# A two-layer decoder step on one core: each weight quarter's products in two passes, high part first

## The chip, the cores and the metric

The kernel runs on one core of a Trainium2 chip. The metric is the device time of the whole launch in microseconds (us), a median of several runs. Engines are named as in the profile: PE is TensorE, PEld its weight load, DVE is VectorE, ACT is ScalarE, POOL is GpSimd, SP is SyncE, which issues most of the transfers.

## What is computed

Two layers of a hybrid decoder trunk for 256 prompt tokens and 8 single decode tokens, 264 token columns in all. Cut to what matters here, a layer is

```
h = rms_norm(x) * norm_w
z = h @ w_in                      # (264, 2048) @ (2048, 7296)
A = rwkv_time_mix(z[:, :3200])    # 12 heads, a recurrent matrix state, a triangular solve per chunk
B = dilated_attention(z[:, 3200:6272])
C = pooling(z[:, 6272:])
x = x + concat(A, B, C) @ w_out   # (264, 2048) @ (2048, 2048)
```

All inputs and outputs are float32.

## The kernel before, in words

**The two large products.** Activations lie with channels on the partitions and the 264 tokens along the free dimension. `stream` (line 301) multiplies them by a group of output tiles of 128 columns, mostly two at a time (`nt` = 2), one PSUM accumulator `acc` for each. The 2048 input channels are taken in four quarters of 512 (loop over `q`), and each quarter in four pieces of 128 (loop over `k4`). To keep float32 accuracy with the faster matmul type, every operand is split into a high part, which is the operand rounded to that type, and a low part, the difference. For a quarter, one transfer brings the weights into `raw` (three buffers, line 294), ACT makes `hi` from it (line 137 is the helper), DVE makes `lo` = `raw` - `hi` (helper, line 140). `hi` and `lo` have two buffers each. For each tile and each piece PE then does three products into the same accumulator: `hi` with the high activations `xh`, `hi` with the low ones `xl`, `lo` with `xh` (line 320). In the output projection the activations are named `mh`, `mb`, `mc` for the high parts and `ml` and others for the low ones. A quarter of a two-tile group is thus 24 matmuls, 12 for each tile, and a layer has 28 such groups and one of a single tile in the input projection (57 tiles) and 8 groups in the output projection: 7008 matmuls in the two layers.

The accumulators come from a PSUM pool `acc` of three banks (line 184, `setup`). A group takes two. When a group ends, DVE reads both (`scaled`, line 326, writes `z`; the output projection's loop in `late` writes `xs`), and the next group's second tile needs the bank that this group's first tile leaves.

**The side work.** Everything else (time mixing, attention, pooling, norms) is small matmuls in the PSUM pool `a` and element work on DVE, ACT and POOL, which is to run beside the streams.

**The order.** The program order written by `Trunk` is not what the engines run. `Plan` (line 1321) reads all instructions, their dependences and the buffers of each pool, gives each a cost, and lists them anew for every engine (`run`, line 1503). An instruction's priority is the length of the longest path behind it (`tails`, line 1478), in which the matmuls of the streams form one chain in program order. An engine takes the ready instruction of highest priority. Side matmuls go ahead of stream matmuls. A matmul whose buffer is not free is set aside and the next ready one is taken (`take`, line 1564). The order found is fixed: each engine then works through its list and waits at semaphores.

The very first group (`begin`) makes its activations quarter by quarter on the way (`first_x`, line 274, four `xh` on ACT and four `xl` on DVE for each quarter).

Of the kernel before, what the change touches and what calls it, by code (L numbers as in the profile page):

```python
# [19 lines left out]
P = 128  # L20
# [3 lines left out]
T = NP + NB  # L24
# [79 lines left out]
class Trunk:  # L104
# [196 lines left out]
    def stream(self, w, c0, nt, xh, xl, order=(0, 1, 2, 3), begin=False):  # L301
        n = nt * P
        accs = [self.ps("acc") for _ in range(nt)]
        for q in order:
            if begin:
                self.first_x(q)
                xh, xl = self.xh, self.xl
            raw = self.early.pop(0) if self.early else self.load(w, c0, n, q)
            hi = self.wpool.tile([P, 4, 256], F32R, tag="hi", name=self.nm("hi"), bufs=2)
            lo = self.wpool.tile([P, 4, 256], F32R, tag="lo", name=self.nm("lo"), bufs=2)  # L310
            self.act(hi[:, :, :n], raw[:, :, :n])
            self.tt(lo[:, :, :n], raw[:, :, :n], hi[:, :, :n].bitcast(F32), ALU.subtract)
            for t in range(nt):
                cs = slice(t * P, (t + 1) * P)
                for k4 in range(4):
                    k = 4 * q + k4
                    o = accs[t][:, :T]
                    first, last = q == order[0] and k4 == 0, q == order[3] and k4 == 3
                    for i, (a, b) in enumerate(((hi[:, k4, cs], xh[k]), (hi[:, k4, cs], xl[k]), (lo[:, k4, cs], xh[k]))):
                        self.nc.tensor.matmul(o, a, b, start=first and i == 0, stop=last and i == 2)  # L320
        return accs

    def project(self, tiles):
# [1439 lines left out]
```

## Time and profile before

| what | value |
|---|---|
| median of 3 runs | 1121.82 us (1119.73 to 1126.0) |
| the profiled execution's own time | 1125.52 us |
| span of that execution | 1123.7 us |
| mean granted TensorE clock, as a share of full speed | 0.977 |
| busy share of the span | PE 94%, PEld 90%, DVE 79%, ACT 49%, POOL 23% |
| stream matmuls (line 320) | 7008 of PE's 9802 |

The span runs from the first to the last instruction. The time of a launch has 1.8 us around it in this execution. PE's matmuls overlap each other, so its busy time counts pipelined work; idle time before an instruction is what its engine waited.

### The profile page before, as it was taken

Reading aid. Unit: us, or ns where it says so; the run is one execution under the profiler, and the core shown is the slowest. Engines: PE = TensorE matmul, PEld = TensorE weight load, DVE = VectorE, ACT = ScalarE, POOL = GpSimd, SP = SyncE. Lnnn points to the kernel's source line nnn. Section 1 sums busy time; section 2 is a strip of 40 time slices with the busy share of each in tenths; the row PEclk is TensorE's granted clock in tenths of the full one; section 3 lists DMA queues with packets and bytes.
Section 4 is the critical chain, followed back from the end, with each engine's and each line's share of the span. In section 5 each row is a group of like instructions: output and inputs, shape, how many; then the busy total and the mean of one; then the engine's idle time right before and its main releaser. Section 6 shows DMA issues by size and latency. Waiting matters only on the chain. (4 is left out here: it accounts for less than half of the span.)

```text
span 1123.7 us, 24664 instructions
## 1 busy us (share of the span) xinstructions
PE 1060.4 (94%) x9802; PEld 1009.0 (90%) x9802; DVE 889.4 (79%) x1665; ACT 545.4 (49%) x928; POOL 258.8 (23%) x391
## 2 busy tenths in 40 slices
PE   8999999889899999999999999988898999989998
PEld 7899999788898897999999999978788999879998
DVE  7668977799997897765675799679899989886444
ACT  6546533345446563444555564334473555634332
POOL 3202310465524111000120132005564321000000
PEclk9999999899999999999999999999898999999999
DMA  7554479866377875576765545897653679456764
GB/s 255 176 166 149 151 251 235 225 151 183 99 214 188 294 231 185 157 232 214 231 214 183 172 132 188 229 251 176 159 172 125 220 242 307 155 167 197 240 219 150
DMA packets 146651, 221.48 MB, mean 197 GB/s; under 512 B 67440, under 2 KB 100608, under 8 KB 146520
## 3 DMA queue, kind: packets, MB, share of 16 engines
q1 hardware_dynamic: 137272, 193.78, 56.9%
q0 software_dynamic: 9264, 26.13, 7.5%
q8 instruction: 77, 1.26, 0.5%
q14 instruction: 38, 0.31, 0.1%
HBM read 197.47 MB, written 22.95 MB: 196 GB/s over the span
## 5 line engine op out<-in xcount | busy, mean ns | idle before, releaser
L320 PE MATMUL acc<-xh,lo 128*128 128x264 f32 x1824 | 534.0, 294 | 27.3 <-DVE lo L140 26.7
L320 PE MATMUL acc<-xh,hi 128*128 128x264 f32 x1824 | 533.0, 293 | 8.2 <-ACT hi L137 7.8
L320 PE MATMUL acc<-xl,hi 128*128 128x264 f32 x1824 | 530.7, 291 | 3.6 <-DVE xl L149 3.6
L137 ACT ACTIVATE hi<-raw 128x1024 fp32r<-128x1024 f32 (+1 forms) x296 | 310.0, 1047 | 408.7 <-PE acc L320 308.0
L140 DVE TENSOR_TENSOR lo<-raw,hi 128x1024 fp32r<-128x1024 f32 (+1 forms) x296 | 361.3, 1221 | 162.1 <-ACT hi L137 159.9
L320 PEld LDWEIGHTS acc<-xh,lo 128*128 128x128 f32 x1824 | 349.8, 192 | 38.8 <-DVE lo L140 33.8
L320 PEld LDWEIGHTS acc<-xh,hi 128*128 128x128 f32 x1824 | 351.4, 193 | 14.4 <-ACT hi L137 8.9
L320 PEld LDWEIGHTS acc<-xl,hi 128*128 128x128 f32 x1824 | 351.3, 193 | 9.7 <-DVE xl L149 4.1
L320 PE MATMUL acc<-mb,hi 128*128 128x264 f32 x384 | 71.8, 283 | 0.0
L140 DVE TENSOR_TENSOR z<-acc,rstd 128x264 f32<-128x264 f32 (+1 forms) x112 | 52.1, 466 | 12.9 <-PE acc L320 12.2
L320 PEld LDWEIGHTS acc<-mb,hi 128*128 128x128 f32 x384 | 59.4, 188 | 0.0
L320 PE MATMUL acc<-mb,lo 128*128 128x264 f32 x192 | 54.6, 284 | 0.0
L320 PE MATMUL acc<-ml,hi 128*128 128x264 f32 x192 | 54.6, 284 | 0.0
L320 PE MATMUL acc<-mh,lo 128*128 128x264 f32 x192 | 54.5, 284 | 0.0
L320 PE MATMUL acc<-mh,hi 128*128 128x264 f32 x192 | 54.4, 283 | 0.0
L350 POOL COPY zcol<-z 128x9 f32<-128x9 f32 x50 | 21.1, 423 | 135.2 <-DVE z L140 132.4
L320 PE MATMUL acc<-mc,hi 128*128 128x264 f32 x256 | 47.6, 284 | 0.0
L320 PEld LDWEIGHTS acc<-mc,hi 128*128 128x128 f32 x256 | 39.7, 188 | 0.0
L320 PE MATMUL acc<-mc,lo 128*128 128x264 f32 x128 | 36.6, 286 | 0.0
L320 PEld LDWEIGHTS acc<-mh,hi 128*128 128x128 f32 x192 | 36.1, 188 | 0.0
L320 PEld LDWEIGHTS acc<-mh,lo 128*128 128x128 f32 x192 | 36.1, 188 | 0.0
L320 PEld LDWEIGHTS acc<-mb,lo 128*128 128x128 f32 x192 | 36.1, 188 | 0.0
(358 smaller groups left out, 1479.9 us busy)
## 6 DMA issues: line engine op xcount, KB each, us to landing
raw<-in_w_in SPq DMA_DIRECT2D x224, 512.0 KB, 3.7
raw<-in_w_out SPq DMA_DIRECT2D x64, 512.0 KB, 3.9
g_dram<-gs SPq DMA_DIRECT2D x8, 768.0 KB
gs<-g_dram SPq DMA_DIRECT2D x8, 768.0 KB
kc<-in_cache_k_w POOLq DMA_DIRECT2D x12, 512.0 KB, 6.6
qb<-q_dram SPq DMA_DIRECT2D x12, 512.0 KB, 5.3
vc<-in_cache_v_w POOLq DMA_DIRECT2D x12, 512.0 KB, 4.8
s<-in_state_wkv POOLq DMA_DIRECT2D x32, 96.0 KB, 4.5
```

The lines of the kernel that those rows point to most:

```text
L137: self.nc.scalar.activation(out, in_, func, **kw)
L140: self.nc.vector.tensor_tensor(out, a, b, op=op)
L320: self.nc.tensor.matmul(o, a, b, start=first and i == 0, stop=last and i == 2)
L350: self.nc.gpsimd.tensor_copy(self.zcol[:, :, a], z[:, NP - 1:T])
```

## The change

The three products of a piece are no longer done together. Within a quarter, a first pass over all tiles of the group does the products with `hi` (two for each piece), and a second pass over all tiles does those with `lo` (one for each piece). The same matmuls run on the same operands; the order of additions in an accumulator changes. The accumulator's start flag goes with the first product of the first pass, its stop flag with the last product of the second.

```
@@ -310,14 +310,15 @@
             lo = self.wpool.tile([P, 4, 256], F32R, tag="lo", name=self.nm("lo"), bufs=2)
             self.act(hi[:, :, :n], raw[:, :, :n])
             self.tt(lo[:, :, :n], raw[:, :, :n], hi[:, :, :n].bitcast(F32), ALU.subtract)
-            for t in range(nt):
-                cs = slice(t * P, (t + 1) * P)
-                for k4 in range(4):
-                    k = 4 * q + k4
-                    o = accs[t][:, :T]
-                    first, last = q == order[0] and k4 == 0, q == order[3] and k4 == 3
-                    for i, (a, b) in enumerate(((hi[:, k4, cs], xh[k]), (hi[:, k4, cs], xl[k]), (lo[:, k4, cs], xh[k]))):
-                        self.nc.tensor.matmul(o, a, b, start=first and i == 0, stop=last and i == 2)
+            parts = ((hi, xh), (hi, xl)), ((lo, xh),)
+            for late, products in zip((False, True), parts):
+                for t in range(nt):
+                    cs = slice(t * P, (t + 1) * P)
+                    for k4 in range(4):
+                        k = 4 * q + k4
+                        for i, (a, b) in enumerate(products):
+                            first = q == order[0] and k4 == 0 and not late and i == 0
+                            self.nc.tensor.matmul(accs[t][:, :T], a[:, k4, cs], b[k], start=first, stop=q == order[3] and k4 == 3 and late)
         return accs
```

## Rows read from the trace of the kernel before

**Rows 1.** The cores, then part 1 of the page: busy time, share, instructions.
```profile
core 0: 1123.7 us, clock 0.977
...
PE 1060.4 (94%) x9802; PEld 1009.0 (90%) x9802; DVE 889.4 (79%) x1665; ACT 545.4 (49%) x928; POOL 258.8 (23%) x391
```

**Rows 2.** The chain that ended last, longest piece: start us, us, what, how many.
```profile
1004.96 115.22 PE acc L320 x948
```

**Rows 3.** Waits of PE: engine and line, for whom: us in total, times, longest.
```profile
PE acc L320 <- DVE lo L140: 26.7, 22, 4.2
PE acc L320 <- ACT hi L137: 7.8, 3, 4.4
PE acc L320 <- DVE xl L149: 3.6, 2, 1.9
...
PE acc L320 <- DVE z L140: 0.3, 2, 0.2
```

**Rows 4.** Waits of all engines, three rows.
```profile
ACT hi L137 <- PE acc L320: 308.0, 176, 9.3
DVE lo L140 <- ACT hi L137: 159.9, 140, 5.1
...
PEld acc L320 <- DVE lo L140: 33.8, 31, 4.4
```

**Rows 5.** Timeline of ACT in the last output projection: start, us, instruction, idle before.
```profile
1035.49 1.06 ACT L137 ACTIVATE hi<-raw 128x1024 fp32r<-128x1024 f32 x1 [1.82 <-PE acc L320]
1038.41 1.06 ACT L137 ACTIVATE hi<-raw 128x1024 fp32r<-128x1024 f32 x1 [1.86 <-PE acc L320]
```

**Rows 6.** Timeline of DVE there.
```profile
1036.59 1.23 DVE L140 TENSOR_TENSOR lo<-raw,hi 128x1024 fp32r<-128x1024 f32 x1 [1.66 <-ACT hi L137]
1037.73 0.42 DVE L140 TENSOR_TENSOR xs<-acc,res 128x264 f32<-128x264 f32 x1
1038.53 0.43 DVE L140 TENSOR_TENSOR xs<-acc,res 128x264 f32<-128x264 f32 x1 [0.38 <-PE acc L320]
```

**Rows 7.** Timeline of PE there: the last matmul of that group.
```profile
1038.21 0.28 PE L320 MATMUL acc<-mh,lo 128*128 128x264 f32 x1
```

**Rows 8.** Waits of PE for lo in 215:310, 575:590 and 765:870 us.
```profile
PE acc L320 <- DVE lo L140: 6.6, 2, 4.2
...
PE acc L320 <- DVE lo L140: 2.2, 1, 2.2
...
PE acc L320 <- DVE lo L140: 8.8, 4, 4.2
```

**Rows 9.** Busy time by stretch: A:B, us, each engine, PEclk, DMA share, GB/s.
```profile
215.00:310.00 95.00, 82.83 (x1273) 76.96 (x1272) 89.88 (x142) 46.47 (x86) 57.75 (x64) 0.93 0.53 148
...
765.00:870.00 105.00, 91.56 (x1340) 85.36 (x1340) 98.15 (x160) 49.77 (x90) 61.99 (x68) 0.92 0.54 154
```

**Rows 10.** Timeline of PE: the end of a long wait.
```profile
304.91 0.59 PE L320 MATMUL acc<-xh,lo 128*128 128x264 f32 x1 [4.15 <-DVE lo L140]
```

**Rows 11.** Timeline of DVE ahead of it.
```profile
295.52 0.17 DVE L149 SCALAR_TENSOR_TENSOR nwt<-nwt,nss 128x24 f32<-128x24 f32 x1
...
296.22 1.02 DVE L149 SCALAR_TENSOR_TENSOR nrs<-nwt,nrs 128x24 f32<-128x24 f32 x1
...
303.65 1.21 DVE L140 TENSOR_TENSOR lo<-raw,hi 128x1024 fp32r<-128x1024 f32 x1
```

**Rows 12.** Timeline of POOL at that time.
```profile
295.68 1.52 POOL L161 TENSOR_TENSOR s<-arows 112x512 f32<-112x512 f32 x1 [0.71 <-DVE asa L152]
```

**Rows 13.** Busy time and clock in short stretches behind long waits for lo.
```profile
218.00:226.00 8.00, 8.00 (x129) 7.63 (x130) 8.00 (x14) 2.88 (x6) 7.57 (x8) 0.57 0.45 141
...
443.00:447.00 4.00, 3.72 (x22) 3.31 (x24) 3.54 (x10) 0.74 (x2) 0.75 (x1) 0.67 0.62 161
...
771.00:775.00 4.00, 3.56 (x81) 3.23 (x85) 4.00 (x9) 1.18 (x3) 3.18 (x4) 0.63 0.36 131
804.00:810.00 6.00, 6.00 (x57) 5.64 (x54) 4.29 (x7) 1.06 (x1) 1.55 (x4) 0.53 0.45 137
```

**Rows 14.** Timeline of PE: the last matmul of a first tile in the input projection.
```profile
109.53 0.28 PE L320 MATMUL acc<-xh,lo 128*128 128x264 f32 x1
```

**Rows 15.** Timeline of DVE: its accumulator is read.
```profile
111.60 0.43 DVE L140 TENSOR_TENSOR z<-acc,rstd 128x264 f32<-128x264 f32 x1
```

## The prediction, on record before the changed kernel ran

> **What bounds the kernel now.** I read the busy shares first, then the chain, then PE's waits, then timelines. PE is busy 94% of the span [rows 1], and the chain that ended last is for its longest piece nothing but the stream: 948 matmuls in 115.22 us, 0.1215 us each [rows 2]. So the kernel is bound by PE, and what can be saved is the time in which PE stands still or runs at the lower clock. Of its standing still, the largest item is the wait for the low weights: 26.7 us in 22 waits, the longest 4.2 us [rows 3]. The waits for the high weights (7.8 us), for `xl` (3.6 us) and for a free accumulator (0.3 us) are small beside it [rows 3]. The weight load that stands before the matmul shows 33.8 us for the same cause [rows 4]; the loss lies between the two, since a matmul's end in the profile overlaps its successor.
>
> Why `lo` comes late is seen in a quiet stretch. A quarter lasts 24 x 0.1215 = 2.92 us, which is the distance of two `hi` there [rows 5]. `hi` has waited 1.8 us for PE: it starts when PE gives a buffer back at the end of a quarter, near 1035.4. It takes 1.06 us, `lo` follows after 1.66 us of waiting for it and ends at 1037.82 [rows 5, 6]. The group's last matmul starts at 1038.21 [rows 7], so the quarter that needs this `lo` starts near 1038.33 and asks for it with its third matmul, at 1038.57. The room is 0.75 us, however idle DVE is. Over the run ACT's `hi` waits 308 us for PE and `lo` 160 us for `hi` [rows 4]: two buffers keep this loop tight everywhere, and any 0.8 us of other work in front of `lo` on DVE stops PE.
>
> **The change, part by part.** No instruction is added or removed: 7008 stream matmuls, as many weight loads, `hi`, `lo` and transfers. At 0.1215 us each the stream takes 851 us in both versions; a tile switch inside a quarter already occurs every 12 matmuls without a gap, so I cost the reordering of matmuls itself at nothing.
>
> *The need for `lo` moves back.* It is asked for by matmul 17 of a quarter instead of matmul 3: 14 x 0.1215 = 1.70 us of cover, always. *`hi` comes free earlier.* Its last reader is 8 matmuls before the quarter's end, 0.97 us, so the next `hi`, and `lo` where DVE is free, start 0.97 us sooner; `lo`'s own buffer and `raw` come free no later. The room in the quiet stretch becomes 0.75 + 1.70 + 0.97 = 3.4 us. What is late next is the high weights where their transfer is late (7.8 us [rows 3]), which stays: SP's list and the number of `raw` buffers are unchanged.
>
> *What the cover is worth.* I split the 26.7 us by stretch. 6.6 us (two waits, 4.2 and 2.4) lie in 215:310 and 8.8 us (four waits, the longest 4.2) in 765:870 [rows 8]; there DVE is busy 89.9 of 95 and 98.2 of 105 us [rows 9]. The other 11.3 us are waits of at most 2.2 us [rows 8], which 1.70 us of cover removes but for 0.5: 10.8 us saved. In the two dense stretches 1.70 us off each wait gives 3.4 + (1.7 + 4.6) = 9.7 us at most. But DVE has only 5.1 + 6.9 = 12 us of idle time there, and PE's side matmuls wait for the same DVE, so between 0 and 9.7 I take half: 4.9 us. For the gap between PE's and the weight load's account (7.1 us) I take half, times the share of waits removed (15.7 of 26.7): 2 us, between 0 and 7.
>
> Why DVE falls behind there is in the rows: an operation of 128x24 that takes 0.17 us alone takes 1.02 us and ends at 297.24, just as a POOL operation that began at 295.68 ends at 297.20 [rows 11, 12]; several such delays add up before the `lo` at 303.65, for which PE waits 4.15 us [rows 10, 11]. The Trainium skill, page "SBUF — State Buffer", section "SBUF: two separate sides", says that VectorE and GpSimd share one port pair as an exclusive lock, and that a VectorE operation with two SBUF inputs is held out while GpSimd reads SBUF. By that rule `lo` itself, with two such inputs, stays exposed; the term of the dense stretches would be 0 instead of 4.9 us and the sum 16 instead of 21.
>
> *The clock.* Behind long waits the granted clock falls to a mean of 0.57, 0.67, 0.63 and 0.53 over 8, 4, 4 and 6 us [rows 13], where full speed is 2.4 GHz and the other level 1.2. The loss is (1 - clock) x length: 3.4 + 1.3 + 1.5 + 2.8 = 9.0 us. Other waits and small matmuls lie there too, so between 0 and 9.0 I take half, 4.5 us.
>
> *What gets worse.* In the first group, `xl` of a quarter's fourth piece is needed by matmul 8 instead of 11. Three matmuls at the lower clock are 0.7 us, in each of the two waits for `xl` [rows 3]: I charge 1 us, between 0 and 1.5. The first tile of a group now ends 4 matmuls before the group's end instead of 12, and the next group's second tile, which needs its bank, starts after 8 instead of 12. The cover for reading the accumulator falls from 24 to 12 matmuls, 2.92 to 1.46 us. In the quiet stretch the first `xs` now runs late because `lo` is in the way until 1037.82 [rows 6]; `lo` will be done earlier, the first tile ends near 1038.0, the read lasts 0.42 and the bank is needed near 1039.3. I charge nothing there; the busy groups are a rival below.
>
> *The new list.* `Plan` lists all engines anew. SP's and POOL's transfers keep their dependences; their places can shift by a matmul or two. I cannot price that from rows and count it in the range.
>
> Sum: 10.8 + 4.9 + 2 + 4.5 - 1 = 21 us. Against the profiled execution's own 1125.5 this is 1104; that execution is 3.7 us above the median of 1121.8, from which it is 1101. I take **1102 us**, near the median. The case's own range is 1092 to 1113.
>
> **The rivals.**
> *The dense stretches give nothing.* DVE stays as late there as POOL makes it, and PE's saved wait returns as a wait of side matmuls for DVE. For it: DVE 95% and 93% busy [rows 9] and the held operation [rows 11, 12]; against it: the stretches have 12 us of idle DVE. Left are 10.8 + 1.5 + 1.3 (the clock behind 443) - 1 = 13 us: 1109. The page's rule named above speaks for this case.
> *Nothing moves.* The engines run `Plan`'s list, not the program. A `lo` that is needed 14 matmuls later has a lower priority, so `Plan` may put other DVE work in front of it until it is as late as before. For it: priorities are path lengths; against it: in the quiet stretch `lo` waits for `hi`, not for DVE [rows 6], so it starts as soon as it can. It also covers the case that the list on PE doesn't follow the two passes. Time 1117 to 1124, 1120 as its middle.
> *Slower: the accumulator's hand-over becomes the wait.* Where DVE has a queue, a first tile whose last matmul starts at 109.53 is read from 111.60 to 112.03 [rows 14, 15]: 2.5 us, against a cover of 1.46 after the change. It decides wherever reading ends later than 1.46 us (1.94 if `Plan` slips the first tile's four low products of the next group forward). If every second of the 56 two-tile groups of the input projection is like that row, PE waits 28 x 1.0 = 28 us more, and with the 20 saved the time is 1130. Against it: reading has a high priority in the list, and the wait is only 0.3 us now [rows 3].
> *More.* All of 33.8 us [rows 4] goes, since the room grew by 2.7 and not 1.7 us, with half of the clock's loss: 37 us after the charge for `xl`, 1085.
>
> **How the numbers follow.** Forecast 0.46, dense stretches give nothing 0.18, nothing moves 0.17, slower by hand-over 0.12, more 0.07. A measurement of this kernel can tell about 0.5%, 5.6 us. The forecast, the first rival and "more" are faster by over 0.5%: 0.71; same 0.17; slower 0.12. The range leaves out the slower case and about half of "more", takes in the bounds of the halved terms and reaches over "nothing moves": 1088 to 1124.
>
> **What would show it.** Right: PE's wait for `lo` falls from 26.7 us to below 10, with what is left in 215:310 and 765:870; ACT's `hi` waits less for PE; in the quiet stretch `lo` ends about a microsecond sooner before its group's end; the mean clock rises above 0.977. The hand-over stays below 3 us. Wrong: PE's waits for `lo` are as long as before, or PE waits for `z` or `xs` by more than 10 us, or side matmuls wait longer by what `lo` lost. A pitch other than 0.1215 us in the last output projection would say that the order of products has a price of its own.

## The result, and the profile after

The changed kernel is slower. Its median is 1137.74 us (1132.77 to 1144.48, four runs), that of the kernel before, with a run more, 1123.47 us (1119.73 to 1126.0). The ratio is 1.0141, with a 95% interval of 1.0101 to 1.0181. The forecast of 1102 us had the wrong sign, and 1137.74 lies outside its range of 1088 to 1124 us. The profiled execution took 1137.24 us, its span is 1135.5 us: 11.8 us more than the span of [rows 1]. The ratios in this document are taken of the undisturbed runs and are not quotients of the medians: two of the versions below had one run each of 1251 and 1256 us, at a granted clock of 0.75, which the ratios leave out.

The cores and part 1 of the page, after:

```profile
core 0: 1135.5 us, clock 0.973
...
PE 1059.8 (93%) x9802; PEld 1013.7 (89%) x9802; DVE 877.8 (77%) x1665; ACT 545.1 (48%) x928; POOL 256.4 (23%) x391
```

PE, DVE, ACT and POOL work no longer than in [rows 1], and PEld 4.7 us longer; PE stands longer and has a slightly lower clock. (1 - clock) x span grew from 25.8 to 30.7 us, and part of that lies in the same waits. What PE waited for, after (engine and line, for whom: us in total, times, longest):

```profile
PE acc L321 <- ACT r L137: 8.9, 2, 4.4
PE acc L321 <- DVE compb L140: 8.4, 5, 2.1
PE a L118 <- DVE ots L140: 7.6, 2, 4.1
PE a L115 <- DMA rt<-i_dram: 5.2, 2, 3.0
...
PE acc L321 <- ACT hi L137: 4.4, 6, 1.2
...
PE acc L321 <- DVE xl L149: 3.7, 2, 1.9
...
PE acc L321 <- DVE z L140: 2.2, 4, 0.7
```

The wait for `lo`, 26.7 us in [rows 3], has no row any more: it is gone altogether, in the dense stretches too. Two things took its place. The stream (`acc`) now waits 8.9 + 8.4 + 2.2 = 19.5 us for operations of the side work and for `z`, which will turn out to be waits for a bank, where [rows 3] has 0.3 us. And the side matmuls (`a`) wait. Adding the idle time before every matmul of the two kinds gives:

| idle time of PE, us | before stream matmuls | before side matmuls | together |
|---|---|---|---|
| before | 39.1 | 20.6 | 59.7 |
| after | 27.7 | 44.3 | 72.0 |

The stream gained 11.4 us and the side work lost 23.7: 12.3 us more idle time, against 11.8 us of span. The waits of ACT and DVE that answer to [rows 4]:

```profile
ACT hi L137 <- PE acc L321: 327.3, 180, 8.4
DVE lo L140 <- ACT hi L137: 141.9, 138, 4.3
```

The quiet stretch went as predicted. Timeline of DVE in the last output projection, after:

```profile
1047.42 1.23 DVE L140 TENSOR_TENSOR lo<-raw,hi 128x1024 fp32r<-128x1024 f32 x1 [1.74 <-ACT hi L137]
1049.69 0.43 DVE L140 TENSOR_TENSOR xs<-acc,res 128x264 f32<-128x264 f32 x1 [1.04 <-PE acc L321]
```

and of PE at the end of that group:

```profile
1049.24 0.90 PE L321 MATMUL acc<-mh,lo 128*128 128x264 f32 x6
```

`lo` ends at 1048.65; the last of these six matmuls starts about 1049.85, five times 0.1215 us after the first. That is 1.2 us ahead of it, against 1038.21 - 1037.82 = 0.4 us before [rows 6, 7]: 0.8 us sooner, where 0.97 was forecast. PE runs at the same speed. Windows of full clock in that stretch, first after, then before (A:B, us, each engine's busy time with its instructions, PEclk, DMA share, GB/s):

```profile
1074.00:1098.00 24.00, 24.00 (x199) 24.00 (x199) 11.99 (x13) 8.50 (x8) 0.00 (x0) 1.00 0.73 232
```
```profile
1034.00:1058.00 24.00, 24.00 (x199) 24.00 (x199) 12.07 (x13) 8.49 (x8) 0.00 (x0) 1.00 0.73 233
```

So the new order of products has no price of its own. The loss starts where a `lo` gets ahead of side work on DVE. Timeline of DVE at the end of a group in the input projection, after, then before:

```profile
71.59 0.43 DVE L140 TENSOR_TENSOR z<-acc,rstd 128x264 f32<-128x264 f32 x1 [1.16 <-PE acc L321]
72.12 1.23 DVE L140 TENSOR_TENSOR lo<-raw,hi 128x1024 fp32r<-128x1024 f32 x1
73.27 0.42 DVE L140 TENSOR_TENSOR z<-acc,rstd 128x264 f32<-128x264 f32 x1
...
75.09 1.22 DVE L140 TENSOR_TENSOR lo<-raw,hi 128x1024 fp32r<-128x1024 f32 x1 [0.87 <-ACT hi L137]
76.23 0.48 DVE L149 SCALAR_TENSOR_TENSOR zk<-z,pr,zk 128x255 f32<-128x255 f32 x1
...
79.54 0.43 DVE L144 TENSOR_SCALAR rs<-a 128x264 f32<-128x264 f32 x1 [0.35 <-PE a L115]
```
```profile
70.31 0.42 DVE L140 TENSOR_TENSOR z<-acc,rstd 128x264 f32<-128x264 f32 x1
71.18 0.43 DVE L140 TENSOR_TENSOR z<-acc,rstd 128x264 f32<-128x264 f32 x1 [0.45 <-PE acc L320]
72.08 1.23 DVE L140 TENSOR_TENSOR lo<-raw,hi 128x1024 fp32r<-128x1024 f32 x1 [0.47 <-ACT hi L137]
73.22 0.87 DVE L149 SCALAR_TENSOR_TENSOR zk<-z,pr,zk 128x255 f32<-128x255 f32 x2
...
76.92 0.43 DVE L144 TENSOR_SCALAR rs<-a 128x264 f32<-128x264 f32 x1 [0.67 <-PE a L115]
```

Before, DVE reads both tiles of the group (`z`), and then comes the `lo`. After, DVE waits 1.16 us for the first tile, which now ends later in its group, and the `lo` is listed before the second `z`. So the second `zk` falls behind the next `lo` as well, and `rs`, which the side chain makes of it (`zk`, its square on ACT, a sum on PE), comes 2.6 us later. By the clock this `lo` is not early (72.12 against 72.08). It is early against the stream, which is 0.9 us behind here (by the times at which equally many stream matmuls have begun). Where DVE is full (57.22 of 60.00 us busy in 97:157 before) the `lo` are early by the clock too. Timeline of DVE there, after, then before:

```profile
108.25 0.48 DVE L149 SCALAR_TENSOR_TENSOR kk<-zk,pr,a 128x264 f32<-128x264 f32 x1
108.65 1.22 DVE L140 TENSOR_TENSOR lo<-raw,hi 128x1024 fp32r<-128x1024 f32 x1
109.78 0.42 DVE L149 SCALAR_TENSOR_TENSOR ta<-ta,kk 128x264 f32<-128x264 f32 x1
```
```profile
104.61 0.48 DVE L149 SCALAR_TENSOR_TENSOR kk<-zk,pr,a 128x264 f32<-128x264 f32 x1
...
105.35 0.42 DVE L149 SCALAR_TENSOR_TENSOR ta<-ta,kk 128x264 f32<-128x264 f32 x1
...
110.47 1.22 DVE L140 TENSOR_TENSOR lo<-raw,hi 128x1024 fp32r<-128x1024 f32 x1
```

This `lo` runs 1.8 us sooner than before and stands between `kk` and `ta`, which grow from 3.6 to 4.4 us late by it. This repeats, and the delays add up. One of the two longest waits for a bank, PE first and then DVE, after:

```profile
130.03 0.56 PE L321 MATMUL acc<-xh,hi 128*128 128x264 f32 x1 [4.42 <-ACT r L137]
```
```profile
127.04 1.22 DVE L140 TENSOR_TENSOR lo<-raw,hi 128x1024 fp32r<-128x1024 f32 x1
128.18 0.48 DVE L149 SCALAR_TENSOR_TENSOR r<-z,pr,r 128x255 f32<-128x255 f32 x1
128.57 0.85 DVE L149 SCALAR_TENSOR_TENSOR bk<-ta,wi 64x256 f32<-64x256 f32 x2
129.45 0.43 DVE L140 TENSOR_TENSOR z<-acc,rstd 128x264 f32<-128x264 f32 x1
```

The waiting matmul opens a new accumulator. No operand of it comes from `r`; it needs the bank that the `z` of 129.45 reads, and it starts 0.15 us after that read has ended. The last matmul into that accumulator had started about 111.3, 18 us earlier, so the cut cover of 1.46 us plays no part in this wait: the accumulator is read late because the side work on DVE, which the list puts around it, is late. All eleven waits in the 19.5 us are for a bank: each of these matmuls starts 0.05 to 0.15 us after DVE has ended a read of an accumulator (`z`, or `compb`, which is taken from one as well). Before, the read that answers to it ended at 125.18, and no PE wait is named there:

```profile
124.77 0.41 DVE L140 TENSOR_TENSOR z<-acc,rstd 128x264 f32<-128x264 f32 x1
```

### The profile page after: what moved, and what is told of

Read it like the earlier page. It is cut to its first block, busy times and chain, and to the rows that moved or that the text cites. A ratio compares the mean times of both kernels' runs of the same rounds, so it can differ in the third digit from the quotient of the medians.

```text
span 1135.5 us, 24662 instructions
## 1 busy us (share of the span) xinstructions
PE 1059.8 (93%) x9802; PEld 1013.7 (89%) x9802; DVE 877.8 (77%) x1665; ACT 545.1 (48%) x928; POOL 256.4 (23%) x391
## 5 line engine op out<-in xcount | busy, mean ns | idle before, releaser
L137 ACT ACTIVATE hi<-raw 128x1024 fp32r<-128x1024 f32 (+1 forms) x296 | 310.2, 1048 | 448.9 <-PE acc L321 327.3
L321 PE MATMUL acc<-xh,hi 128*128 128x264 f32 x1824 | 480.7, 294 | 23.9 <-ACT r L137 8.9
L321 PE MATMUL acc<-xl,hi 128*128 128x264 f32 x1824 | 479.5, 294 | 3.7 <-DVE xl L149 3.7
L321 PE MATMUL acc<-xh,lo 128*128 128x264 f32 x1824 | 284.6, 292 | 0.0
L321 PEld LDWEIGHTS acc<-xh,lo 128*128 128x128 f32 x1824 | 247.8, 193 | 5.0 <-issue 2.3
L321 PE MATMUL acc<-mb,hi 128*128 128x264 f32 x384 | 54.8, 286 | 0.0
L321 PEld LDWEIGHTS acc<-mb,hi 128*128 128x128 f32 x384 | 50.1, 189 | 0.0
L321 PEld LDWEIGHTS acc<-ml,hi 128*128 128x128 f32 x192 | 36.0, 188 | 0.0
L321 PE MATMUL acc<-mc,hi 128*128 128x264 f32 x256 | 34.5, 286 | 0.1
L321 PE MATMUL acc<-mh,lo 128*128 128x264 f32 x192 | 31.4, 286 | 0.0
L321 PE MATMUL acc<-mb,lo 128*128 128x264 f32 x192 | 31.1, 284 | 0.0
```

Source lines behind the costliest of these rows:

```text
L137: self.nc.scalar.activation(out, in_, func, **kw)
L321: self.nc.tensor.matmul(accs[t][:, :T], a[:, k4, cs], b[k], start=first, stop=q == order[3] and k4 == 3 and late)
```

## The experiments

Four explanations were set against each other. **H**, the hand-over: the first tile of a group ends 4 matmuls before the group's end instead of 12, so its bank comes back too late (the prediction's slower rival). **S**, the side chain: `hi` comes free 8 matmuls earlier, so `hi` and `lo` are listed earlier, ahead of side work on a full DVE; everything that hangs on the side work, reads of accumulators included, comes late. **N**, the list: any new list may come out some per cent better or worse for no reason. **L**, the first group's `xl`. All times are medians; each ratio is to the kernel before on the same chip, with its 95% interval.

**1. The orders of before.** The changed program, but DVE, ACT, POOL and SP keep the orders in which they ran before; only PE's list is made anew.

```
+                elif e in lists:
+                    h, k = ready[e], None
+                    if h and h[0][1] == lists[e][turn[e]]:
+                        k = take([heapq.heappop(h)])
+                        turn[e] += k is not None
...
```

> Two passes as in the change, but DVE, ACT, POOL and SP run exactly the lists that the kernel before runs; only PE's list is made anew. Theory S (the new lists put lo 1 to 2 us earlier on DVE and push the side chain's work back where DVE is full, which returns as waits): no displacement is left, PE's wait for lo falls below 12 us as forecast, time 1100 to 1114. Theory H (the bank's hand-over cover, cut from 24 to 12 matmuls, is the loss by itself): the cut is the same as in the change, so PE's waits for banks stay near the change's 20 us, time 1125 to 1140. Theory N (any new list moves the time by a per cent): within 6 us of before, 1118 to 1129.

Measured: 1116.92 us, ratio 0.9943 (0.9909 to 0.9976). Waits of PE:

```profile
PE acc L322 <- ACT hi L138: 14.6, 13, 3.6
PE acc L322 <- DVE lo L141: 9.9, 4, 3.4
PE acc L322 <- DVE compb L141: 4.1, 4, 2.0
```

With the same two passes on PE and the same short hand-over, 21 us of the changed kernel's time are gone, and the kernel is faster than before. So the loss comes in with the order of the other engines, not with PE's. Waits for a bank are 7.4 us, far below the change's 19.5 that H expects. The gain is smaller than S expected; PE waits 14.6 us for `hi` in it. The 9.9 us of waits for `lo` all lie in the two dense stretches, 4.4 us in 215:310 and 5.5 us in 765:870.

**2. The end quarters tile by tile.** In a group's first and last quarter each tile does both of its passes before the other tile, which gives back the hand-over of 24 matmuls.

```
+            todo = [(t, late) for late in (0, 1) for t in range(nt)]
+            if q in (order[0], order[3]):
+                todo = [(t, late) for t in range(nt) for late in (0, 1)]
...
```

> Two passes in the two middle quarters of a group; in its first and last quarter the first tile does both its passes before the second tile begins, so that the first tile ends 12 matmuls before the group's end and the second begins after 12, as before (hand-over cover 24 matmuls again). Lists are made anew. Theory H: the bank waits go, the gain on lo stays, time 1100 to 1112. Theory S: lo is still early in three quarters of four, the side chain still displaced, time 1125 to 1140. Theory N: 1118 to 1135, with waits in other places than in the change.

Measured: 1124.89 us, ratio 1.0004 (0.9981 to 1.0027). H alone is wrong by more than 12 us: the hand-over is whole again, waits for a bank are down to 2.6 us, and the kernel isn't faster than before; PE's idle time before side matmuls is 50.0 us. But it is 12.9 us faster than the changed kernel, so nearly all of the loss goes when the end quarters are done tile by tile. It does not prove S, since it sits at the edge of S's range and inside N's, and it also moves the release of `hi` in half of the quarters.

**3. Three passes.** High by `xh`, then `lo`, then high by `xl`: `lo` is needed 6 matmuls later than before, `hi` is read to the end as before, and the hand-over has only 8 matmuls.

```
-            parts = ((hi, xh), (hi, xl)), ((lo, xh),)
+            parts = ((hi, xh),), ((lo, xh),), ((hi, xl),)
...
```

> Three passes over the tiles in each quarter: hi with xh, lo with xh, hi with xl. lo is needed by matmul 9 instead of 3 (17 in the change), and hi is read until the quarter's end, so it comes free no earlier than before. The first tile ends 4 matmuls before the group's end and the second starts after 4: hand-over cover 8 matmuls, less than the change's 12. Theory S: lo is not early, the side chain is not displaced, a part of the lo waits goes: 1108 to 1120. Theory H: less cover than in the change, so slower than the change or like it: 1135 to 1150. Theory N: anything between 1115 and 1140.

Measured: 1109.53 us, ratio 0.9864 (0.982 to 0.9909). Waits of PE:

```profile
PE acc L320 <- DVE lo L140: 17.8, 19, 3.6
PE acc L320 <- ACT hi L137: 8.2, 6, 3.7
PE acc L320 <- DVE z L140: 6.3, 9, 1.2
```

This version has the shortest hand-over of all and still gains 1.4%, although `lo` is waited for again and waits for a bank are 12.4 us in all (`z` 6.3, `nwt` 4.2 and `compb` 1.8, each as above just after a read). What it has in common with the kernel before is when `hi` comes free. H is out as the main cause: a short hand-over is not enough to make the kernel slower.

**4. Four banks for the accumulators.** In the changed kernel, and, as the experiment's other half, in the kernel before.

```
-  (("acc", 3), ("a", 5))
+  (("acc", 4), ("a", 4))
```

> The change with four accumulator banks instead of three; the side matmuls' pool has four instead of five. Both tiles of the next group then have a bank at once: the cover is a whole group. Theory H: bank waits near 0, time 1100 to 1115 (less what the fifth side bank was worth). Theory S: bank waits near 0 too, but the side chain is as late as in the change, so the waits of side matmuls stay or grow: 1120 to 1135. Theory N: 1115 to 1140.

> The kernel before with four accumulator banks and four side banks: what the trade of banks is worth without the two passes. All theories: the waits for lo stay near 27 us, since the need for lo is unchanged; 1118 to 1130. If it is below 1116, the 1117 of the change with four banks says nothing about the hand-over.

Measured: changed kernel 1117.5 us, ratio 0.9939 (0.991 to 0.9967); kernel before 1111.1 us, ratio 0.9895 (0.9854 to 0.9937). In the changed kernel the stream's waits name only `xl` and `hi` any more; PE's longest rows are now those of side matmuls:

```profile
PE a L115 <- issue: 7.1, 5, 3.0
PE a L115 <- DVE dg L144: 5.0, 2, 2.5
```

A bank more is worth 12 us to the kernel before, which both expectations missed, so 1117.5 alone would mislead: with the hand-over out of the way the change still costs 6.4 us by the medians. The intervals of the two ratios overlap, so this pair alone does not settle the sign; experiment 6 does. S had expected 1120 to 1135 us for the changed kernel, which missed too.

**5. `hi` held in the plan as long as before.** The two passes as in the change, but `Plan` may list a new `hi` only after the last matmul on the `lo` of the same old quarter, thus at the quarter's end, as before. This takes the early release out of the lists and leaves both the late need for `lo` and the short hand-over. (The choice of the tiles is put in words.)

```
+        preds = [set(x) for x in preds]
+        last = [max(k for k in self.touch[t] if stream[k]) for t in <the lo tiles>]
+        for t, k in zip(<the hi tiles>[2:], last):
+            preds[self.touch[t][0]].add(k)
```

> The change with one line of the planning undone: in Plan, hi of a quarter may not be listed before the last matmul (the last one with lo) of the quarter two before it, as if its buffer came free no earlier than in the kernel before. The matmul order, the later need for lo and the cut hand-over cover (12 matmuls) are the change's. Theory S (early hi and lo push the side chain's work on DVE back): the DVE side work in 60 to 180 us is again within 1 us of its times before, where the change had it 2 to 6 us late; the bank waits fall from 20 us to below 8; time 1102 to 1115. Theory H (the cut cover by itself): bank waits as in the change, 1125 to 1140. Theory N (any new list moves the time): no order, 1105 to 1140, with the side work late or early without a pattern.

Measured: 1106.1 us (1099.58 to 1109.62), ratio 0.9842 (0.9789 to 0.9895). Waits of PE, then DVE at the end of the same group:

```profile
PE a L115 <- DVE right L149: 6.5, 2, 3.4
PE acc L321 <- ACT hi L137: 6.4, 3, 3.4
PE acc L321 <- DVE compb L140: 6.2, 4, 1.6
PE acc L321 <- DVE z L140: 5.0, 7, 1.3
...
PE acc L321 <- DVE lo L140: 0.5, 2, 0.2
```
```profile
68.69 0.92 DVE L140 TENSOR_TENSOR z<-acc,rstd 128x264 f32<-128x264 f32 x2 [1.16 <-PE acc L321]
69.53 1.22 DVE L140 TENSOR_TENSOR lo<-raw,hi 128x1024 fp32r<-128x1024 f32 x1
...
75.06 0.43 DVE L144 TENSOR_SCALAR rs<-a 128x264 f32<-128x264 f32 x1 [1.64 <-PE a L115]
```

This is the experiment that decides. A dependence was added to the plan and nothing else, and the kernel became 31.6 us faster than the changed one. DVE waits for the first tile as after the change, but both `z` come before the `lo` again, and `rs` runs at 75.06, 4.5 us sooner than after the change. By 2.9 us of these the stream itself is ahead, from the first three groups on. The dependence acts through the order of the lists, and not by holding the buffer on the chip. Timeline of PE, then ACT, in the last output projection of this version:

```profile
1062.62 1.12 PE L321 MATMUL acc<-mc,lo 128*128 128x264 f32 x8
```
```profile
1062.82 1.06 ACT L137 ACTIVATE hi<-raw 128x1024 fp32r<-128x1024 f32 x1 [1.86 <-PE acc L321]
```

In this quiet stretch `hi` is written during the quarter's eight last matmuls, as in the changed kernel. What costs is thus the early place of `hi` and `lo` in the lists, and the early release on the chip by itself is not shown to cost anything. The wait for `lo` stays away (0.5 us). The waits for banks fell from 19.5 to 11.2 us and not below the expected 8: some of them belong to the short hand-over. The side work was expected within 1 us of its times before; it is 2.6 to 3.4 us early (table below).

**6. `hi` held, and four banks.** Both edits on the changed kernel.

> The same with four accumulator banks and four side banks. Theory S with the bank as the path by which lateness reaches PE: a little better than with three banks, 1098 to 1110, bank waits near 0, and clearly below the 1117 of four banks with early hi. Theory H: the same as four banks with early hi, 1110 to 1120. Theory N: 1105 to 1130.

Measured: 1098.13 us (1096.6 to 1100.27), ratio 0.9779 (0.9736 to 0.9821), the fastest version of all. Its two longest waits of PE:

```profile
PE acc L321 <- ACT hi L137: 7.9, 4, 5.4
PE a L115 <- DVE right L149: 6.2, 2, 3.8
```

The stream's only other row is 1.9 us for `xl`: no wait for a bank and none for `lo` is left on it. With four banks the early listing of `hi` costs 1117.5 - 1098.1 = 19.4 us, with three it cost 31.6: by this difference about 12 us of the cost reach PE by the banks. The banks are a path by which the delay reaches PE, and not its source. In the four-bank pair PE stands 47.5 us before side matmuls with `hi` early and 36.2 us with `hi` held.

**7. Three passes in the first group only** (on the kernel before).

```
+            orders = [[0], [2], [1]] if begin else [[0, 1, 2]]
...
```

> The kernel before, with three passes (hi with xh, lo with xh, hi with xl) in the very first group only. If the 1109.5 of three passes everywhere owes 3.5 us to the first group, where xl is then needed 16 matmuls later, this one shows it alone: PE's wait for xl falls from 3.6 us to about 1 us and the first group ends 3 us sooner, 1117 to 1121. If the gain of three passes came from the later groups alone: 1122 to 1125.

Measured: 1124.09 us, ratio 0.9993 (0.9965 to 1.002). The wait for `xl` fell from 3.6 to 1.0 us as expected and the first group ended some 4 us sooner, but the time stayed: the next group waits 2.1 us for its first `lo`, and at the third group's start the stream is 1.4 us behind the kernel before. L is out as a cause of the loss (the wait for `xl` is 3.7 us after the change and 3.6 before), and a wait saved in the first group alone is no saving. Where `lo` is needed later in all groups, a lead from the start is kept: at 97 us the stream is 3.5 us ahead with three passes and 1.9 us with `hi` held, so a part of those gains comes from there.

**8. Another list for no reason.** `Plan` adds a slack of 350 units to every instruction that doesn't feed the stream; with 300 every list comes out anew, and nothing of the program changes. On the kernel before, the changed one, and the one with `hi` held.

```
-  plan.run(margin=350, ...
+  plan.run(margin=300, ...
```

> The kernel before with its lists made anew for no reason of substance: Plan's margin, the time that it adds to a side instruction's wait for another engine, is 300 ns instead of 350. It measures what a new list alone moves. Theory S: within 0.7% of before, 1116 to 1131, waits for lo still above 18 us. Theory N: it may move by more than 1%, which is the change's loss.

> The change with the same other margin. Theory S: the loss comes from early lo and not from one unlucky list, so it is still above before, or at best like it: 1122 to 1145, with the DVE side work in 60 to 180 us late by 1 us or more. Theory N: anywhere, 1100 to 1140, below before as likely as above.

> The change with hi held back in the lists, and the same other margin. Theory S: the gain stays, 1098 to 1116. Theory N: anywhere, 1100 to 1140.

Measured: 1122.53 us, ratio 1.0008 (0.9972 to 1.0044); 1135.03 us, 1.0101 (1.0031 to 1.0171); 1103.7 us, 0.9832 (0.9767 to 0.9896). The loss and the gain both outlive another list, and a new list alone did nothing to the time that can be measured. It did move waits: in the kernel before with margin 300 PE waits 15.6 us for `lo`, where over 18 were expected, and 35.1 us before side matmuls instead of 20.6. N is out as far as one other list of each version can show it.

**How late the side work is.** For each DVE instruction outside `lo`, its start was compared with that of the same instruction before; medians by when it started before, in us (plus is later):

| started before at | after | before, margin 300 | orders of before | three passes | `hi` held | `hi` held, 4 banks |
|---|---|---|---|---|---|---|
| 20 to 60 | -0.2 | -0.5 | -1.0 | -3.4 | -4.0 | -2.7 |
| 60 to 100 | 2.6 | 0.4 | -1.0 | -3.4 | -2.6 | -4.1 |
| 100 to 140 | 3.6 | 0.4 | -0.6 | -3.7 | -3.1 | -4.4 |
| 140 to 180 | 6.3 | 0.0 | 0.2 | -4.0 | -3.5 | -4.6 |
| 220 to 260 | 10.5 | 0.7 | -1.0 | -1.2 | -1.9 | -5.6 |
| 300 to 340 | 11.1 | 4.3 | -1.5 | -3.2 | -0.2 | -8.8 |

In the same table the `lo` of the changed kernel are at 0.0 us (60 to 100) and -0.8 us (100 to 140), while the side work there is 2.6 and 3.6 us late. The stream is 0.9 us behind up to 97 us; the side work is late beyond that, by itself. Later the stream is held up with it: it is 6.7 us behind at 157. With `hi` listed late, as in three passes and in both versions with `hi` held, the side work is early in every row, whatever the hand-over, and up to 180 us about as early as the stream; with the orders of before it is within 1.5 us of its times. The changed kernel with margin 300 repeats the lateness (1.9 us in 60 to 100, 2.7 in 100 to 140). In experiment 2, with early `hi` but the first tile ending as before, it is 0.1 and 0.2 us there and 3.6 in 220 to 260: the early `lo` and the later end of the first tile make the first lag together. In experiment 7 the side work is 2.5 us late there too, but `lo` with it, and the time is as before, so lateness alone is not the loss. What isn't shown is each single step by which 2.6 us at 76.92 become 11 us at 300; two places were followed row by row, and the rest is read from the table.

## Why the prediction was wrong

**What was right.** The bound and the target: PE's wait for `lo` fell from 26.7 us to nothing. The cover was sized well: with the orders of before (experiment 1) 9.9 us of waits for `lo` are left, all in the dense stretches, where the sum leaves 15.4 - 4.9 = 10.5. In the changed kernel none are left there. The quiet stretch gave 0.8 us of the 0.97 forecast. With the early listing of `hi` taken away, the time falls by 17.4 us where the sum says 21: 1123.5 to 1106.1, by the interval 11.8 to 23.7. That the two are so near is partly luck, since the terms don't agree one by one: in that version PE's idle time before stream matmuls fell by 19.1 us and that before side matmuls grew by 14.8, 4.3 us less together where the terms for waits add up to 17.7, and the clock gave more than its term.

**The step that failed** is "*`hi` comes free earlier* ... start 0.97 us sooner", booked as room and nothing else, together with "*The new list* ... I cannot price that from rows and count it in the range." `lo` doesn't start sooner into nothing: on DVE, 57 of 60 us busy in 97:157 before, a `lo` of 1.2 us that is ready sooner in the plan is listed in front of the side chain. Sign and size: the early listing costs 31.6 us (changed kernel against `hi` held), 14 more than the later need for `lo` gains. The later end of the first tile, which the prediction costed for the bank alone, has its part in it: it is what lets a `lo` get between the two `z` of a group. It could have been asked of the rows: [rows 9] say that DVE is full in places, [rows 4] that `hi` waits 308 us for PE. So what starts a `lo` is mostly PE's release, and an earlier release moves it, in the lists, into DVE time that the side chain was using. The prediction asked who waits for `lo`, and not who waits for DVE behind `lo`.

**Its other terms.** *The dense stretches* (4.9 us, half of 9.7): the stream's waits for `lo` there went to zero and the stream gains in the first of them (from 4.8 us behind the kernel before at 215 us to 1.5 us ahead at 312), but it loses this just behind it (10.5 us behind at 337). The first rival had this in part ("PE's saved wait returns as a wait of side matmuls for DVE"): side matmuls wait 23.7 us longer. It took that as no gain, not as a loss. The rule of the Trainium skill that was set beside it, page "SBUF — State Buffer", section "SBUF: two separate sides", by which `lo` would stay exposed to GpSimd, is not borne out as a wait for `lo` in the changed kernel (no row), and with the orders of before the waits in the dense stretches fall from 15.4 to 9.9 us, where by that rule's sum nothing would be saved there. *The clock* (4.5 us gained): 4.9 us lost, since other long waits came in place of those for `lo`. With `hi` held the mean clock is 0.984 instead of 0.977: (1 - clock) x span falls from 25.8 to 17.7 us there, 8 us, so this term was of the right kind and rather small. *`xl`* (1 us charged): 3.7 us against 3.6, no cost; and experiment 7 shows that a gain in the first group alone is given back. *`hi` waits less for PE*: 327.3 us instead of 308.0, against the forecast; with `hi` held it is 274.4. *No price for reordering the matmuls*: right, 199 in 24 us both times.

**The rivals.** *Nothing moves* argued that a `lo` needed later would have a lower priority; it was listed earlier, as it became ready earlier. *Slower by the hand-over* had the sign, the symptom (the stream waits for a bank: 19.5 us where 28 were priced) and 1130 us, the nearest time. As the main cause it is refuted: with a still shorter hand-over three passes gain 1.4%, and with `hi` held the same hand-over gains 1.6%. The reads behind the longest waits are late because the work around them on DVE is late, not because the cover was cut. But the short hand-over has a price: with three banks, waits for a bank are 7.4 to 12.4 us in experiments 1, 3 and 5, against 0.3 us before. *More* (1085) fails with the forecast.

**The chances** put 0.71 on faster because both effects of the pass order counted as gains. One of them had the opposite sign, and the only case on that side was kept at 0.12 for another cause.

## What to carry to other kernels

Where a list scheduler fills every engine, ask of a change that frees a buffer early what its writer will now be listed ahead of, and whose place on a full engine that takes. A late place in the lists can be kept by one added dependence in the plan while the later need is taken: here that turned 1.4% slower into 1.6% faster, and a fourth accumulator bank made it 2.2%. A wait that names an operation which the waiting instruction doesn't use is followed back to the buffer it needs.

## What the runs showed of the hardware

- The profile's name for a releaser can be that of another operation: 4.42 us of waiting were put down to ACT's `r`, while the matmul started 0.15 us after DVE had read its bank.
- Three banks for the accumulators and five for side matmuls were not the best division, though the kernel before shows only 0.3 us of waits for a bank [rows 3]. Four and four are 1.05% faster (0.63% to 1.46%), and PE's wait for `lo` is then 18.9 us instead of 26.7:

```profile
PE acc L320 <- DVE lo L140: 18.9, 23, 2.3
```
